# Seven products in place of eight in the FFN's first matmul of a two-layer trunk

## The chip, the core and the metric

The kernel runs on one core of a Trainium2 chip. The metric is the device time of one execution in microseconds; the time given for a kernel is the median of its runs. A profile belongs to one more execution, taken by the hardware profiler. In it PE is TensorE's matmuls, PEld its weight loads, DVE VectorE, ACT ScalarE, POOL GpSimd, and SP the engine whose queue issues most transfers.

## The reference

Two layers of attention and a gated FFN on 512 tokens of width 1024, all in float32. The change is in the FFN of each layer and in the final norm behind it:

```python
    h2 = rms_norm(x, g_ffn)
    gate, up = jnp.split(h2 @ w_ffn_in, 2, axis=-1)       # 1024 -> 2 x 2816
    return x + (jax.nn.silu(gate) * up) @ w_ffn_out       # 2816 -> 1024
...
    return rms_norm(x, norm_final)
```

## The kernel before

Everything is held transposed: channels on the 128 partitions, the 512 tokens along the free axis. The residual x is eight tiles `xs[0..7]` of 128 x 512. To keep float32 precision each operand is split in a rounded part and a remainder (`hi`, `lo`, fp32r), and each contraction tile takes three matmuls (`mm_tiles`, L205 to L207): hi by hi, lo by hi, hi by lo, all into one PSUM bank of 512 columns.

Weights come in one stream (`stream`, in the order of `layer_order`, L82 and L83). For each weight tile `w_pieces` issues a transfer of 512 KB on SP's queue into `wr` (three buffers), a cast on ScalarE into `wh` (L111) and a subtraction on VectorE into `wl` (L113; four buffers each). `w_get` hands out the next tile and keeps two ahead (`W_AHEAD`).

After attention the output projection adds into `xs`, and `Norm.feed` makes the scaled `hh` and `hl` of each tile and sums its squares; the reciprocal root r (one value a token) comes later from `Norm.finish`, and is multiplied in behind the matmuls, since it commutes with them. Then, in each layer:

- The FFN's first product (L623 to L640): 22 hidden tiles j, each with a gate product `fg` and an up product `fu` of 8 contraction tiles x 3 matmuls of 512 columns. VectorE multiplies both by r (L632, L634), ScalarE applies silu (L633), GpSimd multiplies (L635), and ScalarE and VectorE split the result into `ah` and `al` (L638, L639). All 22 pairs are kept.
- The FFN's second product (L644 to L651): output tiles m, each 22 contraction tiles x 3 matmuls into one bank, the weights in three tiles (1024, 1024 and 768 columns); VectorE adds the bank into `xs[m]` (L648).
- In the last layer output tile 7 is made in three stretches of 256, 128 and 128 tokens (L654 to L673). Behind each come the squares, two `ones_d` matmuls for the mean square (L666, L667), the reciprocal root (L152 to L156), eight multiplications on VectorE and GpSimd (L672) and the stores (L673).

Banks go round by `fbank` through eight PSUM banks. Each engine takes its instructions from a queue in order; the order across the program is made by a planner that follows the program's order of issue and its own estimate of when operands are there. The inputs' layout is made on the host, outside the time.

Of the kernel before, what the change touches and what calls it, by code (L numbers as in the profile page):

```python
# [35 lines left out]
BANK_BUFS = dict(mm=3, at=5)  # L36
W_BUFS, W_AHEAD = 4, 2
GATES_IN_BLK = 4
FILL = (3, 3, 3, 3, 4, 4, 4, 4)
LAG = 2  # L40


def f32(ap):
    return ap.bitcast(F32)
# [3 lines left out]
def trunk(ctx: ExitStack, tc, xT, par, tab, scn, msk, w_in, w_o, w_out, w_fi, w_fo, out):  # L48
# [7 lines left out]
    def bank(tag, name):  # L56
        return psm.tile([P, 512], F32, name=name, tag=tag, bufs=BANK_BUFS[tag])
# [24 lines left out]
    layer_order += [("fi", j) for j in range(2 * NH)]  # L82
    layer_order += [("fo", m, c) for m in range(8) for c in range(3)]  # L83
    stream = [(l,) + k for l in range(DEPTH) for k in layer_order]

    def w_src(k):
        l, kind, i = k[:3]
        if kind == "fo":
            c0, c1 = k[3] * 1024, min(k[3] * 1024 + 1024, HID)
            return w_fo[l, i][:, c0:c1]  # L90
        return {"in": w_in, "o": w_o, "out": w_out, "fi": w_fi}[kind][l, i]

    ready = []
# [2 lines left out]
    def w_pieces(*steps):  # L96

        n = state["next"]
        state["next"] = n + 1
        src = w_src(stream[n])  # L100
        cols = src.shape[1]
        raw = wp.tile([P, 1024], F32, name=f"wr{n}", tag="wr", bufs=3)
        hi = wp.tile([P, 1024], F32R, name=f"wh{n}", tag="wh", bufs=W_BUFS)
        lo = wp.tile([P, 1024], F32R, name=f"wl{n}", tag="wl", bufs=W_BUFS)
        ready.append((stream[n], hi, lo))
        at = 0
        for n_cols in steps:
# [6 lines left out]
            yield  # L114

    def w_prefetch():
        for _ in w_pieces(1024):
            pass

    def w_get(*key):  # L120
        while len(ready) <= W_AHEAD and state["next"] < len(stream):
            w_prefetch()
        k, hi, lo = ready.pop(0)
        assert k == key, (k, key)
        return hi, lo
# [69 lines left out]
    def mm(dst, key, rhs, first=True, last=True):  # L195

        hi, lo = w_get(*key)
        mm_tiles(dst, hi, lo, rhs, first, last)

    def mm_tiles(dst, hi, lo, rhs, first, last, c0=0):  # L200
        n = len(rhs)
        for k in range(n):
            rh, rl = rhs[k]
            c = slice((c0 + k) * P, (c0 + k + 1) * P)
            nc.tensor.matmul(dst, hi[:, c], rh, start=first and k == 0, stop=False)  # L205
            nc.tensor.matmul(dst, lo[:, c], rh, start=False, stop=False)  # L206
            nc.tensor.matmul(dst, hi[:, c], rl, start=False, stop=last and k == n - 1)  # L207
# [61 lines left out]
    def fbank(name):  # L269
        t = free_tags[fcount[0] % len(free_tags)]  # L270
        fcount[0] += 1
        return bank(t, name)

    for l in range(DEPTH):
        h = nrm.h
        with ExitStack() as ac:
# [337 lines left out]
            for m in range(8):  # L614
# [2 lines left out]
                nc.vector.tensor_tensor(out=xs[m], in0=b, in1=xs[m], op=ALU.add)  # L617
                nrm.feed(m)
        h = nrm.h
        with ExitStack() as fc:  # L620
            fp = fc.enter_context(tc.tile_pool(name=f"ffn{l}", bufs=1))
            act = []
            for j in range(NH):  # L623
                bg = fbank(f"fg{j}_{l}")
                mm(bg, (l, "fi", 2 * j), h)
                bu = fbank(f"fu{j}_{l}")
                mm(bu, (l, "fi", 2 * j + 1), h)
                if j == 0:
                    r = nrm.finish()
                g = fp.tile([P, S], F32, name=f"g{j}_{l}", tag="g", bufs=3)  # L630
                u = fp.tile([P, S], F32, name=f"u{j}_{l}", tag="u", bufs=3)
                nc.vector.tensor_tensor(out=g, in0=bg, in1=r, op=ALU.mult)  # L632
                silu = nc.scalar.activation(out=g, in_=g, func=AF.Silu)  # L633
                nc.vector.tensor_tensor(out=u, in0=bu, in1=r, op=ALU.mult)  # L634
                nc.gpsimd.tensor_tensor(out=u, in0=u, in1=g, op=ALU.mult)  # L635
                hi = fp.tile([P, S], F32R, name=f"ah{j}_{l}", tag="a", bufs=2 * NH)
                lo = fp.tile([P, S], F32R, name=f"al{j}_{l}", tag="a", bufs=2 * NH)
                nc.scalar.copy(out=hi, in_=u)  # L638
                nc.vector.tensor_tensor(out=lo, in0=u, in1=f32(hi), op=ALU.subtract)  # L639
                act.append((hi, lo))  # L640
            table(LNEXP, silu)
            last = l == DEPTH - 1
            nrm = Norm(C_NL if last else C_NA + 8 * (l + 1), f"a{l + 1}", split=not last)
            for m in range(7 if last else 8):  # L644
                b = fbank(f"fo{m}_{l}")
                for c in range(3):
                    mm(b, (l, "fo", m, c), act[8 * c:8 * c + 8], c == 0, c == 2)
                nc.vector.tensor_tensor(out=xs[m], in0=b, in1=xs[m], op=ALU.add)  # L648
                nrm.feed(m)
                if last:  # L650
                    nc.scalar.activation(out=xs[m], in_=xs[m], func=AF.Copy, scale=pt[:, C_NL + m:C_NL + m + 1])  # L651
            if last:

                w7 = [w_get(l, "fo", 7, c) for c in range(3)]  # L654
                for t, (t0, t1) in enumerate(((0, 256), (256, 384), (384, 512))):
                    ts, n = slice(t0, t1), t1 - t0
                    b = fbank(f"fo7{t}")
                    for c, (hi, lo) in enumerate(w7):
                        a = [(u[:, ts], v[:, ts]) for u, v in act[8 * c:8 * c + 8]]
                        mm_tiles(b[:, :n], hi, lo, a, c == 0, c == 2)  # L660
                    x7 = xs[7][:, ts]
                    nc.vector.tensor_tensor(out=x7, in0=b[:, :n], in1=x7, op=ALU.add)
                    sq = fp.tile([P, n], F32, name=f"sq7{t}", tag="g", bufs=3)
                    nc.scalar.activation(out=sq, in_=x7, func=AF.Square)
                    ms = bank("at", f"ms7{t}")
                    nc.tensor.matmul(ms[:, :n], ones_d, nrm.acc[:, ts], start=True, stop=False)  # L666
                    nc.tensor.matmul(ms[:, :n], ones_d, sq, start=False, stop=True)  # L667
                    nc.scalar.activation(out=x7, in_=x7, func=AF.Copy, scale=pt[:, C_NL + 7:C_NL + 8])
                    r = rsqrt_of(lambda name: rp.tile([P, n], F32, name=name, tag="r"), ms[:, :n], f"z{t}")
                    for m in range(8):  # L670
                        eng = nc.gpsimd if m in (0, 2, 4) else nc.vector
                        eng.tensor_tensor(out=xs[m][:, ts], in0=xs[m][:, ts], in1=r, op=ALU.mult)  # L672
                        (nc.scalar if m % 2 else nc.sync).dma_start(out=out[m][:, ts], in_=xs[m][:, ts])  # L673

# [52 lines left out]
```

## Time and profile before

| | us |
|---|---|
| runs of the kernel before: median (lowest to highest of 3) | 1513.78 (1513.16 to 1515.3) |
| the profiled execution | 1513.47 |
| span of its instructions | 1511.6 |
| TensorE busy in the span | 1484.6 |
| VectorE, ScalarE, GpSimd busy | 843.6, 615.5, 336.7 |

A matmul's duration in the records is modelled and covers its passage through the array; matmuls overlap, so what one costs in a run of them is the distance between two starts. A wait is put down to the semaphore that came last.

### The profile page before, as it was taken

Reading aid. Unit: us, or ns where it says so; the run is one execution under the profiler, and the core shown is the slowest. Engines: PE = TensorE matmul, PEld = TensorE weight load, DVE = VectorE, ACT = ScalarE, POOL = GpSimd, SP = SyncE. Lnnn points to the kernel's source line nnn. Section 1 sums busy time; section 2 is a strip of 40 time slices with the busy share of each in tenths; the row PEclk is TensorE's granted clock in tenths of the full one; section 3 lists DMA queues with packets and bytes.
Section 4 is the critical chain, followed back from the end, with each engine's and each line's share of the span. In section 5 each row is a group of like instructions: output and inputs, shape, how many; then the busy total and the mean of one; then the engine's idle time right before and its main releaser. Section 6 shows DMA issues by size and latency. Waiting matters only on the chain.

```text
span 1511.6 us, 17712 instructions
## 1 busy us (share of the span) xinstructions
PE 1484.6 (98%) x6954; PEld 1237.3 (82%) x6954; DVE 843.6 (56%) x1020; ACT 615.5 (41%) x974; POOL 336.7 (22%) x222
## 2 busy tenths in 40 slices
PE   9899999999999999999998999999999999999997
PEld 7788888888888888888876878888888888888887
DVE  6978776575454545432358776665645454443223
ACT  6556554643322233322345655446343333332321
POOL 2464652001111111101124454510021111110111
PEclk9999999999999999999999999999999999999999
DMA  6122232233223232333321123322322223233321
GB/s 251 44 79 66 78 101 81 71 110 98 98 98 98 92 103 86 97 93 105 110 82 57 63 78 98 98 70 87 109 98 84 100 95 98 97 94 93 100 77 57
DMA packets 44772, 139.61 MB, mean 92 GB/s; under 512 B 5776, under 2 KB 9232, under 8 KB 44688
## 3 DMA queue, kind: packets, MB, share of 16 engines
q1 hardware_dynamic: 42816, 137.39, 28.1%
q10 hardware_dynamic: 1872, 1.09, 0.2%
q8 instruction: 55, 0.90, 0.2%
q14 instruction: 29, 0.24, 0.1%
HBM read 132.16 MB, written 2.10 MB: 89 GB/s over the span
## 4 chain that ended last, share of the span: by engine, by line
PE 89%; DVE 5%; ACT 2%; issue 1%; DMA 1%; POOL 1%; SPq 1%; DVEq 0%; POOLq 0%; ACTq 0%
PE fo L205 5%; PE fo L206 5%; PE fo L207 5%; PE fg L206 5%; PE fu L206 5%; PE fu L205 5%; PE fg L205 5%; PE fu L207 5%; PE fg L207 5%; PE pg L205 4%; PE pg L206 4%; PE pg L207 4%; PE pd L205 2%; PE pd L206 2%; PE pd L207 2%; PE wo L207 2%
## 5 line engine op out<-in xcount | busy, mean ns | idle before, releaser
L111 ACT CAST wh<-wr 128x1024 fp32r<-128x1024 f32 (+3 forms) x251 | 258.1, 1029 | 632.1 <-issue 186.4
L113 DVE TENSOR_TENSOR wl<-wr,wh 128x1024 fp32r<-128x1024 f32 (+2 forms) x229 | 327.4, 1430 | 208.3 <-ACT wh L111 207.9
L635 POOL TENSOR_TENSOR u<-u,g 128x512 f32<-128x512 f32 x44 | 56.8, 1291 | 441.5 <-DVE u L634 394.3
L205 PE MATMUL fo<-ah,wh 128*128 128x512 f32 (+2 forms) x396 | 146.8, 371 | 0.0
L206 PE MATMUL fo<-ah,wl 128*128 128x512 f32 (+2 forms) x396 | 146.8, 371 | 0.0
L207 PE MATMUL fo<-al,wh 128*128 128x512 f32 (+2 forms) x396 | 146.7, 370 | 0.0
L205 PE MATMUL fg<-hhf,wh 128*128 128x512 f32 x352 | 137.7, 391 | 0.0
L207 PE MATMUL fu<-hlf,wh 128*128 128x512 f32 x352 | 136.9, 389 | 0.0
L206 PE MATMUL fg<-hhf,wl 128*128 128x512 f32 x352 | 136.9, 389 | 0.0
L207 PE MATMUL fg<-hlf,wh 128*128 128x512 f32 x352 | 136.9, 389 | 0.0
L205 PE MATMUL fu<-hhf,wh 128*128 128x512 f32 x352 | 136.9, 389 | 0.0
L206 PE MATMUL fu<-hhf,wl 128*128 128x512 f32 x352 | 136.9, 389 | 0.0
L634 DVE TENSOR_TENSOR u<-fu,yf 128x512 f32<-128x512 f32 x44 | 30.4, 691 | 129.2 <-PE fu L207 129.2
L205 PE MATMUL pg<-hha,wh 128*128 128x512 f32 x256 | 101.0, 394 | 0.0
L207 PE MATMUL pg<-hla,wh 128*128 128x512 f32 x256 | 100.2, 392 | 0.0
L206 PE MATMUL pg<-hha,wl 128*128 128x512 f32 x256 | 100.2, 391 | 0.0
L207 PEld LDWEIGHTS fo<-al,wh 128*128 128x128 f32 x396 | 74.6, 188 | 13.0
L206 PEld LDWEIGHTS fo<-ah,wl 128*128 128x128 f32 x396 | 74.6, 188 | 12.9
L205 PEld LDWEIGHTS fo<-ah,wh 128*128 128x128 f32 x396 | 74.6, 188 | 12.9
L205 PEld LDWEIGHTS fg<-hhf,wh 128*128 128x128 f32 x352 | 66.1, 188 | 14.3 <-issue 0.5
L206 PEld LDWEIGHTS fg<-hhf,wl 128*128 128x128 f32 x352 | 66.1, 188 | 14.0 <-issue 0.5
L207 PEld LDWEIGHTS fu<-hlf,wh 128*128 128x128 f32 x352 | 66.1, 188 | 13.7
(270 smaller groups left out, 3067.0 us busy)
## 6 DMA issues: line engine op xcount, KB each, us to landing
wr<-in_w_fi_dram SPq DMA_DIRECT2D x88, 512.0 KB, 3.3
wr<-in_w_in_dram SPq DMA_DIRECT2D x78, 512.0 KB, 3.3
wr<-in_w_fo_dram SPq DMA_DIRECT2D x32, 512.0 KB, 3.5
wr<-in_w_o_dram SPq DMA_DIRECT2D x16, 512.0 KB, 3.4
wr<-in_w_out_dram SPq DMA_DIRECT2D x16, 512.0 KB, 3.3
wr<-in_w_fo_dram SPq DMA_DIRECT2D x16, 384.0 KB, 3.1
x<-in_xT_dram SPq DMA_DIRECT2D x8, 256.0 KB, 5.9
cs<-in_tab_dram SPq DMA_DIRECT2D x2, 512.0 KB, 4.3
```

The lines of the kernel that those rows point to most:

```text
L111: nc.scalar.copy(out=hi[:, c], in_=raw[:, c])
L113: state["wl"] = eng.tensor_tensor(out=lo[:, c], in0=raw[:, c], in1=f32(hi[:, c]), op=ALU.subtract)
L205: nc.tensor.matmul(dst, hi[:, c], rh, start=first and k == 0, stop=False)
L206: nc.tensor.matmul(dst, lo[:, c], rh, start=False, stop=False)
L207: nc.tensor.matmul(dst, hi[:, c], rl, start=False, stop=last and k == n - 1)
L634: nc.vector.tensor_tensor(out=u, in0=bu, in1=r, op=ALU.mult)
L635: nc.gpsimd.tensor_tensor(out=u, in0=u, in1=g, op=ALU.mult)
```

## The change

In eleven of the 22 hidden tiles of each layer (`FAST`: 3, 5, 7, 8, 10, 11, 13, 14, 16, 17, 19) gate and up are computed together as a 2 x 2 block product: two output blocks (gate, up) by two halves of the tokens (`H` = 256 columns), over two halves of the contraction (even and odd tiles of 128 channels: `EVEN_ODD`, for which the host permutes the rows of `w_fi`). The Strassen-Winograd scheme makes the four results from seven block products and sums.

- Sums of the activations, once a layer: for four pairs of tiles, two scalings on ScalarE, three sums of 256 columns on VectorE and one on GpSimd, then one cast and one subtraction of 1024 columns (`sh`, `sl`).
- Sums of the weights, for each fast tile (`w_sums`): the two transfers of 512 KB as before, four subtractions of 512 columns on GpSimd in a chain (result `tf`, one buffer), and casts and subtractions of three tiles of 1024 and one of 512 columns, where an ordinary hidden tile has two of 1024. A fast tile counts as two in the look-ahead.
- The products (`Fast`, `prod`): 4 contraction tiles x 3 matmuls of 256 columns each. The bank `r0` takes b11 a11, then t2 s2, then t3 s3, then t4 a22, each on top of the last, and ScalarE copies it out after each of the first three (`snap`); `r2` takes t1 s1 and later b22 s4; `r1` takes b21 a12. VectorE adds copies to banks to make gate and up, GpSimd multiplies half of the gate by r. The last two products (`tail`) run after the first product of the next tile.
- The product of silu and up reads the up bank in PSUM on VectorE in an ordinary tile (no multiplication by r), and runs on GpSimd in a fast one. r is multiplied in behind the second product instead (`add_x`, two VectorE operations where one was).
- The second product goes in parts of the hidden tiles (`CHUNKS`): 0 to 5 after hidden tile 6, 6 to 11 after hidden tile 12, and 12 to 21 (two weight tiles of 640 columns, `ENDS`) at the end. Each part is added into `xs` by itself. Fourteen buffers hold `ah` and `al` where 44 did.
- In the last layer output tiles 6 and 7 are made in two halves of 256 tokens, in place of tile 7 alone in 256, 128 and 128.

The core of the diff:

```diff
+CHUNKS = ((0, 6), (6, 12), (12, 17), (17, NH))
+ENDS = (2, 3)
+FAST = (3, 5, 7, 8, 10, 11, 13, 14, 16, 17, 19)
+EVEN_ODD = (0, 2, 4, 6, 1, 3, 5, 7)
...
+    def w_sums():
...
+        pool, tag, bufs = (wp, "wr", 3) if j % 2 else (fp, "wx", 2)
+        rg = pool.tile([P, 2, 512], F32, name=f"rg{n}", tag=tag, bufs=bufs)
+        ru = pool.tile([P, 2, 512], F32, name=f"ru{n}", tag=tag, bufs=bufs)
+        for t, i in ((rg, 2 * j), (ru, 2 * j + 1)):
+            nc.sync.dma_start(out=t.rearrange("p a k -> p (a k)"), in_=w_fi[l, i])
+        tf = fp.tile([P, 3, 512], F32, name=f"tf{n}", tag="tf", bufs=1)
...
+        g = parts(rg, wp, "wh", W_BUFS, [P, 2, 512])
+        tt(nc.gpsimd, tf[:, 0], ru[:, 0], rg[:, 0])
+        tt(nc.gpsimd, ru[:, 0], ru[:, 1], ru[:, 0])
+        tt(nc.gpsimd, tf[:, 1], ru[:, 1], tf[:, 0])
+        tt(nc.gpsimd, tf[:, 2], rg[:, 1], tf[:, 1])
+        t = parts(tf[:, 0:2], fp, "ta", 2, [P, 2, 512])
+        u = parts(ru, wp, "wh", W_BUFS, [P, 2, 512])
+        v = parts(tf[:, 2], fp, "tb", 2, [P, 512])
...
+            for i in range(4):
+                he, ho = F("g", f"he{i}", 2), F("u", f"ho{i}", 2)
...
+                nc.vector.tensor_tensor(out=sf[:, 0], in0=he[:, H:], in1=ho[:, H:], op=ALU.add)
+                nc.gpsimd.tensor_tensor(out=sf[:, 2], in0=he[:, :H], in1=he[:, H:], op=ALU.subtract)
+                nc.vector.tensor_tensor(out=sf[:, 1], in0=sf[:, 0], in1=he[:, :H], op=ALU.subtract)
+                nc.vector.tensor_tensor(out=sf[:, 3], in0=ho[:, :H], in1=sf[:, 1], op=ALU.subtract)
...
+            def prod(dst, w, a, first=False):
+                hi, lo = w
+                for k, (ah, al) in enumerate(a):
+                    c = slice(k * P, k * P + P)
+                    for x, y, n in ((hi, ah, 0), (lo, ah, 1), (hi, al, 2)):
+                        nc.tensor.matmul(dst, x[:, c], y, start=first and k + n == 0,
+                                         stop=n == 2 and k == len(a) - 1, skip_group_check=True)
...
+                def __init__(self, j):
...
+                    prod(self.r0, self.w["b11"], A["a11"], True)
+                    self.a = self.snap("a")
...
+                def middle(self):
...
+                    prod(self.r2, w["t1"], A["s1"], True)
+                    prod(self.r0, w["t2"], A["s2"])
+                    b = self.snap("b")
+                    prod(r1, w["b21"], A["a12"], True)
...
+                    nc.vector.tensor_tensor(out=self.g[:, :H], in0=r1, in1=self.a, op=ALU.add)
+                    nc.gpsimd.tensor_tensor(out=self.g[:, :H], in0=self.g[:, :H], in1=r[:, :H], op=ALU.mult)
+                    prod(self.r0, w["t3"], A["s3"])
+                    c = self.snap("c")
+                    nc.vector.tensor_tensor(out=self.u[:, H:], in0=self.r2, in1=c, op=ALU.add)
...
+                def tail(self):
+                    w = self.w
+                    prod(self.r0, w["t4"], A["a22"])
+                    nc.vector.tensor_tensor(out=self.g[:, H:], in0=self.r0, in1=r[:, H:], op=ALU.mult)
+                    prod(self.r2, w["b22"], A["s4"])
+                    nc.vector.tensor_tensor(out=self.u[:, :H], in0=self.r2, in1=self.b, op=ALU.add)
+                    return hidden(self.j, self.g, self.u)
...
+            def add_x(b, m, ts=slice(0, S)):
...
+                nc.vector.tensor_tensor(out=t, in0=b, in1=r[:, ts], op=ALU.mult)
+                nc.vector.tensor_tensor(out=x, in0=t, in1=x, op=ALU.add)
...
+                for t, (t0, t1) in enumerate(((0, H), (H, S))):
...
+                    for m in (6, 7):
...
+                        eng = nc.gpsimd if m in ((0, 2, 3, 5, 6), (0, 2, 4))[t] else nc.vector
```

## Rows read from the trace of the kernel before

**Rows 1.** The page, first part: busy time, share of the span, instructions.

```profile
PE 1484.6 (98%) x6954; PEld 1237.3 (82%) x6954; DVE 843.6 (56%) x1020; ACT 615.5 (41%) x974; POOL 336.7 (22%) x222
```

**Rows 2.** The page, fourth part: the chain that ended last, by engine.

```profile
PE 89%; DVE 5%; ACT 2%; issue 1%; DMA 1%; POOL 1%; SPq 1%; DVEq 0%; POOLq 0%; ACTq 0%
```

**Rows 3.** Stretch: length, busy us of PE, PEld, DVE, ACT, POOL; clock, DMA.

```profile
391.92:424.56 32.64, 32.64 (x144) 26.68 (x143) 16.85 (x19) 12.79 (x16) 2.59 (x2) 1.00 0.29 92
60.00:520.00 460.00, 454.11 (x2164) 379.40 (x2163) 293.52 (x367) 212.57 (x360) 128.30 (x75) 1.00 0.27 86
1478.45:1486.37 7.92, 7.92 (x68) 7.91 (x67) 1.38 (x2) 1.35 (x2) 0.00 (x0) 1.00 0.01 2
```

**Rows 4.** Timeline of TensorE (start, duration): 24 matmuls of 512 columns apart.

```profile
561.44 0.39 PE L205 MATMUL fu<-hhf,wh 128*128 128x512 f32 x1
...
566.88 0.39 PE L205 MATMUL fg<-hhf,wh 128*128 128x512 f32 x1
```

**Rows 5.** The same: first matmul of layer 0's FFN, first of layer 1.

```profile
391.92 0.39 PE L205 MATMUL fg<-hhf,wh 128*128 128x512 f32 x1
...
751.84 0.39 PE L205 MATMUL p<-hha,wh 128*128 128x512 f32 x1
```

**Rows 6.** The same: 66 matmuls of 256 columns; 21 of 128.

```profile
1478.45 0.28 PE L205 MATMUL fo<-ah,wh 128*128 128x256 f32 x1
...
1486.37 0.59 PE L666 MATMUL ms<-acca,ones_d 128*128 128x256 f32 x2
...
1487.08 0.27 PE L205 MATMUL fo<-ah,wh 128*128 128x128 f32 x1
...
1489.42 0.27 PE L205 MATMUL fo<-ah,wh 128*128 128x128 f32 x1
```

**Rows 7.** Timeline of the end: last FFN matmul; final multiplications of two parts.

```profile
1492.55 3.38 DVE L672 TENSOR_TENSOR x<-x,yz 128x256 f32<-128x256 f32 x5
...
1502.25 0.27 PE L207 MATMUL fo<-al,wh 128*128 128x128 f32 x1
...
1506.83 1.88 DVE L672 TENSOR_TENSOR x<-x,yz 128x128 f32<-128x128 f32 x5
```

**Rows 8.** The page, sixth part: transfers of FFN weights, size, us to landing.

```profile
wr<-in_w_fi_dram SPq DMA_DIRECT2D x88, 512.0 KB, 3.3
```

**Rows 9.** Groups by line and shape: busy, mean ns of one, idle before.

```profile
L111 ACT CAST wh<-wr 128x1024 fp32r<-128x1024 f32 x230 | 242.1, 1053 | 563.2 <-issue 186.4 <-PE fg L207 113.8 <-PE fo L207 89.5
L635 POOL TENSOR_TENSOR u<-u,g 128x512 f32<-128x512 f32 x44 | 56.8, 1291 | 441.5 <-DVE u L634 394.3 <-ACT g L633 47.2
L632 DVE TENSOR_TENSOR g<-fg,yf 128x512 f32<-128x512 f32 x44 | 30.4, 692 | 65.4 <-PE fg L207 65.3
...
L664 ACT ACTIVATE sq<-x 128x256 f32<-128x256 f32 x1 | 0.4, 417 | 6.2 <-DVE x L662 6.2
L662 DVE TENSOR_TENSOR x<-fo,x 128x256 f32<-128x256 f32 x1 | 0.4, 425 | 5.8 <-PE fo L207 5.8
L672 POOL TENSOR_TENSOR x<-x,yz 128x256 f32<-128x256 f32 x3 | 2.7, 935 | 25.5 <-DVE yz L156 25.5
```

**Rows 10.** Waits of TensorE (total, times, longest), and the tile waited for.

```profile
PE avs L469 <- DVE tls L438: 6.7, 6, 2.2
...
L438 DVE TENSOR_TENSOR tls<-ts,ths x48: 402/676/693, 78.0 to 912.7; 128x512 fp32r<-128x512 f32 x32, 128x256 fp32r<-128x256 f32 x16
```

**Rows 11.** Timeline of GpSimd and VectorE in an ordinary hidden tile.

```profile
567.94 1.29 POOL L635 TENSOR_TENSOR u<-u,g 128x512 f32<-128x512 f32 x1 [9.59 <-DVE u L634]
...
568.21 2.10 DVE L113 TENSOR_TENSOR wl<-wr,wh 128x1024 fp32r<-128x1024 f32 x1 [0.44 <-ACT wh L111]
...
573.65 1.23 DVE L113 TENSOR_TENSOR wl<-wr,wh 128x1024 fp32r<-128x1024 f32 x1 [0.44 <-ACT wh L111]
```

**Rows 12.** The same two at the start of the FFN.

```profile
383.47 0.75 DVE L174 SCALAR_TENSOR_TENSOR hlf<-x,pt,hhf 128x512 fp32r<-128x512 f32 x1
...
383.52 1.84 POOL L188 TENSOR_TENSOR accf<-accf,sqf 128x512 f32<-128x512 f32 x1 [3.60 <-ACT sqf L186]
```

More of the change, by code (lines that the diff above doesn't have):

```diff
@@ L81, in trunk @@
     layer_order += [("o", m) for m in range(8)] + [("out", m) for m in range(8)]
-    layer_order += [("fi", j) for j in range(2 * NH)]
-    layer_order += [("fo", m, c) for m in range(8) for c in range(3)]
+    FFN = []
+    for j in range(NH):
+        FFN.append(("j", j))
+        FFN += [("c", c) for c, (j0, j1) in enumerate(CHUNKS) if j1 == j and c not in ENDS]
+    for kind, i in FFN:
+        if kind == "c":
+            layer_order += [("fo", m, i) for m in range(8)]
+        elif i not in FAST:
+            layer_order += [("fi", 2 * i), ("fi", 2 * i + 1)]
+        else:
+            layer_order.append(("fs", i))
+    layer_order += [("fo", m, c) for c in ENDS for m in range(2)] + [("fo", m, c) for m in range(2, 8) for c in ENDS]
     stream = [(l,) + k for l in range(DEPTH) for k in layer_order]
@@ L120, in w_get @@
     def w_get(*key):
-        while len(ready) <= W_AHEAD and state["next"] < len(stream):
+        while state["next"] < len(stream):
+            ahead = sum(2 if r[0][1] == "fs" else 1 for r in ready[1:])
+            if ready and ahead >= W_AHEAD:
+                break
             w_prefetch()
@@ L619, in trunk @@
         h = nrm.h
+        nrm_f = nrm
         with ExitStack() as fc:
[L621 to L632, printed above, removed]
-                silu = nc.scalar.activation(out=g, in_=g, func=AF.Silu)
[L634 to L640, printed above, removed]
@@ new lines, in trunk, with hidden @@
+            act = {}
+            last = l == DEPTH - 1
+            def hidden(j, g, u):
+                silu = nc.scalar.activation(out=g, in_=g, func=AF.Silu)
+                p = F("p", f"p{j}", 2)
+                (nc.vector if u.space == bass.MemoryType.PSUM else nc.gpsimd).tensor_tensor(
+                    out=p, in0=u, in1=g, op=ALU.mult)
+                if j < NH - 3:
+                    hi, lo = F("a", f"ah{j}", 14, dt=F32R), F("a", f"al{j}", 14, dt=F32R)
+                else:
+                    tag, bufs = (("tah", 2), ("tal", 2), ("sh0", 1))[j - NH + 3]
+                    t = F(tag, f"ae{j}", bufs, (P, 2, S), F32R)
+                    hi, lo = t[:, 0], t[:, 1]
+                nc.scalar.copy(out=hi, in_=p)
+                nc.vector.tensor_tensor(out=lo, in0=p, in1=f32(hi), op=ALU.subtract)
+                act[j] = (hi, lo)
+                return silu
@@ new lines, in add_x @@
+            def add_x(b, m, ts=slice(0, S)):
+                x = xs[m][:, ts]
+                t = F("p", f"ft{m}", 2)[:, ts]
+                nc.vector.tensor_tensor(out=t, in0=b, in1=r[:, ts], op=ALU.mult)
+                nc.vector.tensor_tensor(out=x, in0=t, in1=x, op=ALU.add)
+            late = []
+            for kind, i in FFN:
+                if kind == "j" and i not in FAST:
+                    bg = fbank(f"fg{i}_{l}")
+                    mm(bg, (l, "fi", 2 * i), hq)
+                    for o in late:
+                        silu = o.tail()
+                    late = []
+                    bu = fbank(f"fu{i}_{l}")
+                    mm(bu, (l, "fi", 2 * i + 1), hq)
+                    if i == 0:
+                        r = nrm_f.finish()
+                    g = F("g", f"g{i}", 2)
+                    nc.vector.tensor_tensor(out=g, in0=bg, in1=r, op=ALU.mult)
+                    silu = hidden(i, g, bu)
+                elif kind == "j":
+                    f = Fast(i)
+                    for o in late:
+                        o.tail()
+                    f.middle()
+                    late = [f]
+                else:
+                    for m in range(8):
+                        b = fbank(f"fo{m}{i}_{l}")
+                        mm(b, (l, "fo", m, i), [act[j] for j in range(*CHUNKS[i])])
+                        add_x(b, m)
@@ L641, in trunk, with finished @@
+            assert not late
             table(LNEXP, silu)
-            last = l == DEPTH - 1
             nrm = Norm(C_NL if last else C_NA + 8 * (l + 1), f"a{l + 1}", split=not last)
[L644 to L649, printed above, removed]
-                if last:
-                    nc.scalar.activation(out=xs[m], in_=xs[m], func=AF.Copy, scale=pt[:, C_NL + m:C_NL + m + 1])
+            def finished(m, ts=slice(0, S), square=True):
+                if square:
+                    nrm.feed(m)
+                if last:
+                    x = xs[m][:, ts]
+                    nc.scalar.activation(out=x, in_=x, func=AF.Copy, scale=pt[:, C_NL + m:C_NL + m + 1])
@@ new lines, in trunk @@
+            head = [fbank(f"fo{m}e_{l}") for m in range(2)]
+            for i in ENDS:
+                for m, b in enumerate(head):
+                    mm(b, (l, "fo", m, i), [act[j] for j in range(*CHUNKS[i])], i == ENDS[0], i == ENDS[-1])
+            for m in range(6 if last else 8):
+                if m < 2:
+                    b = head[m]
+                else:
+                    b = fbank(f"fo{m}e_{l}")
+                    for i in ENDS:
+                        mm(b, (l, "fo", m, i), [act[j] for j in range(*CHUNKS[i])], i == ENDS[0], i == ENDS[-1])
+                add_x(b, m)
+                finished(m)
@@ L652, in trunk @@
             if last:
-                w7 = [w_get(l, "fo", 7, c) for c in range(3)]
-                for t, (t0, t1) in enumerate(((0, 256), (256, 384), (384, 512))):
+                ws = {(m, i): w_get(l, "fo", m, i) for m in (6, 7) for i in ENDS}
+                for t, (t0, t1) in enumerate(((0, H), (H, S))):
                     ts, n = slice(t0, t1), t1 - t0
[L657 to L669, printed above, removed]
@@ new lines, in trunk @@
+                    for m in (6, 7):
+                        b = fbank(f"fo{m}{t}")[:, :n]
+                        for i in ENDS:
+                            a = [(act[j][0][:, ts], act[j][1][:, ts]) for j in range(*CHUNKS[i])]
+                            mm_tiles(b, *ws[m, i], a, i == ENDS[0], i == ENDS[-1])
+                        add_x(b, m, ts)
+                        sq = F("p", f"sq{m}{t}", 2)[:, :n]
+                        nc.scalar.activation(out=sq, in_=xs[m][:, ts], func=AF.Square)
+                        if m < 7:
+                            acc = nrm.acc[:, ts]
+                            nc.vector.tensor_tensor(out=acc, in0=acc, in1=sq, op=ALU.add)
+                            finished(m, ts, False)
@@ L670, in trunk @@
+                    ms = bank("at", f"ms7{t}")[:, :n]
+                    nc.tensor.matmul(ms, ones_d, nrm.acc[:, ts], start=True, stop=False)
+                    nc.tensor.matmul(ms, ones_d, sq, start=False, stop=True)
+                    finished(7, ts, False)
+                    rz = rsqrt_of(lambda name: rp.tile([P, n], F32, name=name, tag="r"), ms, f"z{t}")
                     for m in range(8):
-                        eng = nc.gpsimd if m in (0, 2, 4) else nc.vector
-                        eng.tensor_tensor(out=xs[m][:, ts], in0=xs[m][:, ts], in1=r, op=ALU.mult)
@@ L673, in trunk @@
-                        (nc.scalar if m % 2 else nc.sync).dma_start(out=out[m][:, ts], in_=xs[m][:, ts])
+                        eng = nc.gpsimd if m in ((0, 2, 3, 5, 6), (0, 2, 4))[t] else nc.vector
+                        eng.tensor_tensor(out=xs[m][:, ts], in0=xs[m][:, ts], in1=rz, op=ALU.mult)
+                        (nc.scalar if m % 2 and t else nc.sync).dma_start(out=out[m][:, ts], in_=xs[m][:, ts])
 def _tiles(np, w, kt, nt):
```

50 lines of the change are left out of this document (47 added, 3 removed).

## The prediction

> **What bounds the kernel now.** I read the page first: TensorE is busy 98% of the span while VectorE is at 56% and GpSimd at 22% [rows 1], and the chain that ended last lies on TensorE for 89% [rows 2]. Then the busy times by stage: in the first three hidden tiles of a layer TensorE is busy for all 32.64 us, VectorE for 16.85, ScalarE for 12.8, GpSimd for 2.6 [rows 3]. So in this stage the kernel is as fast as its matmuls follow one another, and only fewer or shorter matmuls help. The pace comes from the timeline, as the distance of starts (the durations shown are modelled and overlap). With 512 columns, 24 matmuls take from 561.44 to 566.88: 0.2267 us each [rows 4]; a layer's whole FFN, 391.92 to 751.84, holds 1584 matmuls and gives 0.2272 [rows 5], so nothing stalls there. With 256 columns, in the first part of output tile 7, 66 matmuls take 1478.45 to 1486.37: 0.120 us. With 128 columns 21 take 2.34 us: 0.111 [rows 6]. So half the columns cost 53% and a quarter 49%.
>
> **The change, term by term.** The sum starts at the profiled run, 1513.47 us, which lies 0.3 under the median of the runs.
>
> **Seven products.** An ordinary hidden tile has 2 x 8 x 3 = 48 matmuls of 512 columns: 48 x 0.2267 = 10.88 us. A fast one has 7 products of 4 contraction tiles, three matmuls each, of 256 columns: 84 x 0.120 = 10.08 us. That is 0.80 us for each of 22 fast tiles: -17.6 us. An eighth fewer columns would be 1.36 us; the rest goes to the 13 ns that each matmul costs above its columns at 2.4 GHz (0.120 against 256/2.4 = 0.107, 0.2267 against 0.2133), now paid 84 times, not 48. The granted clock is 1.00 in the FFN and in the stretch of 256 columns alike [rows 3], the upper of its two levels. By the Trainium skill (TensorE: Matmul & The Clock Gate, Back-to-back issue gap: N/2.4 + 2.5 ns) the saving would be 48 x 215.8 - 84 x 109.2 ns = 1.19 us a tile, 26 in all. The rows show 11 ns more at both widths, so I keep 17.6.
>
> **The end.** Before, output tiles 6 and 7 of the last layer take from 1478.45 - 66 x 0.2267 = 1463.49 to the last product's end at about 1502.36 [rows 6, 7]: 38.9 us, most of it 132 matmuls of 128 columns at the price of 256. Now 72 of their matmuls go to the early parts at 512 columns (16.3 us), the rest is 120 of 256 columns (14.4), and about 1.0 of the mean-square products stands between: 31.7. That is -7.2 us. What follows the last product was 1511.6 - 1502.4 = 9.2 us on 128 columns and is now on 256: the five multiplications of VectorE 3.38 us, not 1.88 [rows 7]; one more VectorE operation of 0.42; by 1.04 ns a column (0.692 against 0.425 us for 512 and 256 in the groups of costs below) 0.13 more for the first and for each of three operations of the reciprocal root; estimated in the same way, 0.1 for each of ScalarE's three, 0.3 for the mean-square matmuls and 0.2 for the last store. Sum 1.5 + 0.42 + 0.5 + 0.3 + 0.3 + 0.2 = +3.2 us (2 to 4).
>
> **The second FFN product in parts.** The matmuls are the same in number and width. It adds, for each output tile, part sums into the residual: three times two VectorE operations of 0.69 where one was. In the first two parts an output tile lasts 18 x 0.2267 = 4.1 us on TensorE and asks VectorE for 1.4 us and one weight remainder, narrower than an ordinary tile's; so it is hidden. There are 32 weight transfers a layer where there were 24, all smaller; two ahead is 6.8 us of TensorE (2 x 15 matmuls) in the last part against 3.3 us to landing [rows 8] and at most 2.3 of splitting (a cast and a remainder of 1024 columns, 1.05 and 1.23, in the groups below): hidden, cost 0. Without that cover each part tile would wait up to 5.6 - 3.4 = 2.2 us.
>
> **Short reads between products.** Three products of a fast tile accumulate on the same bank, and ScalarE copies the bank out in between (0.42 us for 256 columns, as VectorE's [rows 9]). After the first copy two or three other products follow; the second copy has one product (12 x 0.120 = 1.44 us) of cover, the third one product when a fast tile follows and the 5.4 us of a gate product when an ordinary one does. If ScalarE is just inside a cast of 1024 columns (1.05 us [rows 9]) the copy is late: 1.05 + 0.42 and the hand-over either way exceed 1.44. The queue is in order, so a cast that waits there for GpSimd also holds the copy; and on TensorE the waiting product holds all that is queued behind it. The trace has no such read; the nearest are the evacuations of the transposes in attention, of which TensorE waited for 6 of 48, 6.7 us in all, 0.14 us each [rows 10]. I take that for two tight reads of each fast tile: 44 x 0.14 = +6.2 us. Bounds: 0 (the product between covers all), and 1.5 us a fast tile, 33.
>
> **Start of the stage.** The sums of the activations are made while hidden tiles 0 to 2 run. VectorE was busy 16.85 of these 32.64 us [rows 3]; now come four times three operations of 0.42 and a remainder of 1.23 [rows 11], 10.0, and 1.9 for the remainders of a fast tile's weights in place of an ordinary one's: 28.7. ScalarE goes from 12.8 to about 24.5 (eight scalings of 512 columns at an estimated 0.7, between the 0.42 and the 1.05 of rows 9; four casts of 1.05; the extra weight casts 1.7). GpSimd has 8 us: four differences of a fast tile's weights at 1.29 and four of the activations at 0.7. So each fits, but if VectorE and GpSimd exclude each other all the time, 36.7 us do not, and the first fast tile is 4 us late. I take 1 us a layer, +2 us (0 to 8).
>
> **Steady load.** A fast tile asks ScalarE for about 6.2 of 10.08 us, no bound. VectorE: three remainders of 1.23 and two of 0.69, all with both inputs in SBUF, 5.07 us, and four operations from PSUM of 0.42, 1.7 us. GpSimd: four differences of 512 columns and one product at 1.29, and one of 256 columns (between 0.65, half of it, and 0.94 [rows 9]; I take 0.7), 7.15 us. An ordinary tile asks VectorE for 3.1 and 1.4 us and GpSimd for nothing, since its product now reads PSUM on VectorE. Two fast and an ordinary give TensorE 31.04 us, VectorE 18.0, GpSimd 14.3: each alone has room, so cost 0 on throughput. The weights of a fast tile are the same two transfers of 512 KB on SP's queue, which now start together. But the two don't run side by side: a remainder that takes 1.23 us takes 2.10 when GpSimd works beside it [rows 11], and GpSimd's 1.29 becomes 1.84 behind VectorE [rows 12]. The Trainium skill (SBUF — State Buffer, Who interferes with whom) says that a VectorE instruction with two SBUF inputs and a GpSimd instruction that reads SBUF exclude each other for a whole instruction, and one with a single SBUF input does not. The first half agrees with the 0.87 us added here; the second no row here shows.
>
> **Sum:** 1513.5 - 17.6 - 7.2 + 3.2 + 6.2 + 2 = 1500.1, so **1500 us**. Without any stall it is 1491.9.
>
> **Rivals.** *A, VectorE and GpSimd become the bound* because of that exclusion. In two fast tiles and an ordinary one 14.3 + 2 x 5.07 + 3.1 = 27.5 us exclude each other and 4.7 are VectorE's alone. If these never fall beside GpSimd's work the group needs 32.3 us against TensorE's 31.04: 1.2 us, some 11 groups, 13 us. With the stalls above: 1500 + 13 = 1513, no change. For it: the four differences are a chain and have one buffer for their results, so late work can't be made up early. Against it: VectorE's PSUM reads can lie beside GpSimd, and the two long early parts of the second FFN product let the queue empty. *B, slower:* the copies out of the bank stand behind casts that wait for that chain. A lost turn at the port costs one remainder, 1.23 us; if every fast tile loses one and TensorE waits it out, beside the 0.28 taken above, the stage pays 22 x 1.23 = 27 us: 1500 + 27 = 1527. It turns slower than before from 21.6/22 = 0.98 us of stall a fast tile. For it: one in-order queue holds both, and TensorE has 1.44 us of cover. Against it: the same engines feed attention and TensorE is busy 454 of 460 us there [rows 3]. *C, half the columns cost half* between products that change banks: 0.113 in place of 0.120, 22 x 84 x 7 ns = 12 us less, 1488. Against it: the 66 matmuls of rows 6 have the same form and a new weight tile each time. *D, the products are not fewer in effect:* if the order given to TensorE left it waiting for as long as it saves, only the end's 4.0 us would remain, 1509.5; that is the forecast's upper edge, no case of its own.
>
> **How the numbers follow.** Forecast (stalls from 0 to 0.8 us a fast tile, 1490 to 1510.5) 0.70; A 0.12; B 0.15; C 0.03. The range leaves out C and most of B: 1490 to 1517. A measurement of this kernel can tell some 0.2%, 3 us, from no change. Faster by more (under 1510.8): forecast, C and a part of A that has overlap, 0.78; the same 0.07; slower 0.15.
>
> **What would show it.** In the profile after: 12 matmuls of a product 1.44 us apart; the fast stretch with TensorE 95% busy or more and its waits on ScalarE's copies some 6 us in all; the remainders of VectorE near 2 us where GpSimd works; GpSimd busy about 70% there; after the last product some 12.4 us. I am wrong if the groups of two fast tiles and an ordinary one take much over 32 us, if the first fast tile starts late by several us, or if weights arrive late in the parts of the second product.

## The result, and the profile after

The changed kernel takes 1498.76 us (median; 1496.57 to 1500.28) against 1514.05 of the kernel before in the same runs: a ratio of 0.9899, 95% interval 0.9885 to 0.9913, so 1.0% less. The forecast was 1500. Its profiled execution took 1496.57 us, 16.9 under that of the kernel before, and its spans can be set side by side by stage. Each bound is the start of the first matmul of the next stage; the last stage begins where the first matmul of the last mean square follows the last product.

| stage, us | before | after | difference |
|---|---|---|---|
| start and attention of layer 0 | 391.92 | 390.99 | -0.93 |
| FFN of layer 0 | 359.92 | 351.53 | -8.39 |
| attention of layer 1 | 381.65 | 385.15 | +3.50 |
| FFN of layer 1, to its last product | 368.87 | 353.16 | -15.71 |
| from the last product to the end | 9.24 | 13.97 | +4.73 |
| span | 1511.6 | 1494.8 | -16.8 |

The bounds of layer 0's FFN after, as in [rows 5] before:

```profile
390.99 0.39 PE L259 MATMUL fg<-hhf,wh 128*128 128x512 f32 x1
...
742.52 0.39 PE L259 MATMUL p<-hha,wh 128*128 128x512 f32 x1
```

The first stage is the same code in both; its length lies between 391.0 and 393.3 us in the profiles of this case, so its difference says nothing. The sum of the forecast had 8.2 us of stalls in the FFN that are not there, and lacked 1.5 us at the end and 3.5 us of a stage that it left out. That it came out within 2 us is luck, since these cancel; the points below take it apart.

The page of the kernel after, first part and the granted clock of its second part:

```profile
PE 1461.4 (98%) x7670; PEld 1253.0 (84%) x7670; DVE 976.0 (65%) x1229; ACT 691.8 (46%) x1122; POOL 483.0 (32%) x317
...
PEclk9999999999999999999999999999999999999998
```

It answers [rows 1]: 716 more matmuls, yet TensorE is busy 23 us less; GpSimd does 146 us more, VectorE 132, ScalarE 76. The busy times by stretch (columns as in [rows 3]), first the three hidden tiles at the start of layer 0's FFN, then 40 us with fast and ordinary tiles:

```profile
391.00:423.60 32.60, 32.60 (x144) 26.66 (x142) 27.92 (x37) 22.94 (x30) 8.69 (x8) 1.00 0.35 114
600.00:640.00 40.00, 40.00 (x288) 37.84 (x287) 24.99 (x31) 16.82 (x26) 21.75 (x15) 1.00 0.24 80
```

TensorE is busy without a gap in both, as in [rows 3]. The waits of TensorE in the whole of layer 0's FFN, 391 to 742 us, are an empty list; so are those in layer 1's FFN up to 1480. What comes between the reads is seen in TensorE's timeline (the first matmul of each run, start and duration):

```profile
424.50 0.28 PE L725 MATMUL fa<-hhf,whh 128*128 128x256 f32 x1
...
425.94 0.28 PE L725 MATMUL fc<-sh,tah 128*128 128x256 f32 x1
...
427.38 0.28 PE L725 MATMUL fb<-hhf,whh 128*128 128x256 f32 x1
...
428.82 0.40 PE L259 MATMUL fg<-hhf,wh 128*128 128x512 f32 x1
429.05 0.28 PE L725 MATMUL fa<-sh,tah 128*128 128x256 f32 x1
...
430.49 0.40 PE L260 MATMUL fg<-hhf,wl 128*128 128x512 f32 x1
...
435.96 0.28 PE L725 MATMUL fa<-sh,whh 128*128 128x256 f32 x1
```

Each product of 12 matmuls lasts 1.44 us, as reckoned. But `fa`, the bank that ScalarE copies, is not taken up in the order of the code: the planner has put `fb` forward and the gate product of an ordinary tile (`fg`) in between. So in this first fast tile 3.1 us pass between the first and the second product on that bank (425.94 to 429.05), and 5.5 us between the second and the third (430.49 to 435.96), where the code order gives 1.44 for either. Over the 22 fast tiles the shortest such time is 2.88 us, two products.

### The profile page after: what moved, and what is told of

It is laid out like the page before. It is cut to its first block, busy times and chain, and to the rows that moved or that the text cites. A ratio compares the mean times of both kernels' runs of the same rounds, so it can differ in the third digit from the quotient of the medians.

```text
span 1494.8 us, 19780 instructions
## 1 busy us (share of the span) xinstructions
PE 1461.4 (98%) x7670; PEld 1253.0 (84%) x7670; DVE 976.0 (65%) x1229; ACT 691.8 (46%) x1122; POOL 483.0 (32%) x317
## 3 DMA queue, kind: packets, MB, share of 16 engines
q1 hardware_dynamic: 45120, 137.91, 28.7%
## 4 chain that ended last, share of the span: by engine, by line
PE 87%; DVE 6%; ACT 3%; issue 1%; POOL 1%; DMA 1%; SPq 0%; DVEq 0%; POOLq 0%; ACTq 0%
PE fa L725 8%; PE fc L725 4%; PE pg L259 4%; PE pg L260 4%; PE pg L261 4%; PE fo L259 3%; PE fo L260 3%; PE fo L261 3%; PE fg L259 3%; PE fg L260 3%; PE fu L261 3%; PE fg L261 3%; PE fu L260 3%; PE fu L259 3%; PE fb L725 2%; PE wo L259 2%
## 5 line engine op out<-in xcount | busy, mean ns | idle before, releaser
L127 ACT CAST wh<-wr 128x1024 fp32r<-128x1024 f32 (+4 forms) x223 | 213.8, 964 | 327.5 <-issue 55.3
L129 DVE TENSOR_TENSOR wl<-wr,wh 128x1024 fp32r<-128x1024 f32 (+3 forms) x201 | 247.6, 1236 | 77.4 <-ACT wh L127 75.9
L259 PE MATMUL fo<-ah,wh 128*128 128x512 f32 (+1 forms) x220 | 82.8, 376 | 0.0
L260 PE MATMUL fo<-ah,wl 128*128 128x512 f32 (+1 forms) x220 | 82.6, 375 | 0.0
L261 PE MATMUL fo<-al,wh 128*128 128x512 f32 (+1 forms) x220 | 82.3, 376 | 0.0
L259 PE MATMUL pd<-hha,wh 128*128 128x512 f32 x192 | 76.4, 398 | 0.3 <-ACT knd3s L404 0.3
L260 PE MATMUL pd<-hha,wl 128*128 128x512 f32 x192 | 76.2, 397 | 0.0
L261 PE MATMUL pd<-hla,wh 128*128 128x512 f32 x192 | 76.0, 396 | 0.0
L259 PE MATMUL fg<-hhf,wh 128*128 128x512 f32 x176 | 69.1, 393 | 0.0
L260 PE MATMUL fu<-hhf,wl 128*128 128x512 f32 x176 | 68.6, 390 | 0.0
```

## The experiments

**No fast tile.** All else of the change stays.

```diff
-FAST = (3, 5, 7, 8, 10, 11, 13, 14, 16, 17, 19)
+FAST = ()
...
-            for i in range(4):
+            for i in range(4 if FAST else 0):
```

> No hidden tile is fast; all else of the change stays (parts of 6, 6 and 10, last tiles by halves); the sums of the activations, which nothing reads then, are left out. If the seven products are worth their pace, 0.80 us a tile, and stand without stalls: FFN of layer 0 back from 351.5 to 360 us, the run 17 us above the changed kernel, near 1514. If stalls of 0.28 us a fast tile were in the changed kernel, only 0.52 a tile comes back: FFN of layer 0 at 357, the run near 1508. If the gain came from the parts of the second product, layer 0's FFN stays under 355.

Measured: 1512.02 us (median), ratio to before 0.9987 (0.9977 to 0.9996); the profiled span is 1510.0. Layer 0's FFN is 359.92, to the last digit that of the kernel before (start of its first matmul and of the next stage's first):

```profile
392.64 0.39 PE L259 MATMUL fg<-hhf,wh 128*128 128x512 f32 x1
...
752.56 0.39 PE L259 MATMUL p<-hha,wh 128*128 128x512 f32 x1
```

Layer 1's FFN is 361.53 where the changed kernel has 353.16. So eleven fast tiles are worth 8.39 and 8.37 us, 0.76 a tile where 0.80 was reckoned: the first theory, without stalls. The parts of the second product cost and give nothing in layer 0. In layer 1 the FFN without fast tiles is 7.34 us shorter than before: that is the end in two halves, reckoned at 7.2. Attention of layer 1 is 381.98 here, 3.2 less than in the changed kernel, though nothing in it was touched.

**Own buffers at the end.**

```diff
-rsqrt_of(lambda name: rp.tile([P, n], F32, name=name, tag="r"), ms, f"z{t}")
+rsqrt_of(lambda name: fp.tile([P, n], F32, name=name, tag="gu"[name[0] == "t"], bufs=2), ms, f"z{t}")
```

> Only the buffers of the last reciprocal root change: each half has its own pair, so that the second half's root no longer waits for the first half's five multiplications on GpSimd. If that wait is what made the end 4.7 us longer where 3.2 were reckoned, the time from the last product to the end falls from 14.0 by 1.4 (GpSimd still has the first half's work) to 2.3 us. If the end is long because of the stores or the wider operations alone, it stays at 14.0.

Measured: 1495.18 us (median); the end takes 11.83 us, not 13.97, all other stages but the first within 0.1 of the changed kernel's. In the changed kernel VectorE's queue at the end, and GpSimd's, read:

```profile
1487.20 0.42 DVE L208 SCALAR_TENSOR_TENSOR tz<-yz 128x256 f32<-128x256 f32 x1 [1.97 <-POOL x L847]
...
1483.12 4.05 POOL L847 TENSOR_TENSOR x<-x,yz 128x256 f32<-128x256 f32 x5 [13.80 <-DVE yz L210]
```

and with own buffers

```profile
1485.54 0.42 DVE L208 SCALAR_TENSOR_TENSOR tz<-yz 128x256 f32<-128x256 f32 x1 [2.19 <-ACT yz L207]
...
1480.36 4.26 POOL L847 TENSOR_TENSOR x<-x,yz 128x256 f32<-128x256 f32 x5 [10.60 <-DVE yz L210]
```

The second half's root starts on VectorE when GpSimd is through with the first half (1483.12 + 4.05), because the tag `r` has two buffers and each root takes two; with buffers of its own it starts when its operand is there.

**Which weights GpSimd splits.** The input projection's weights go to GpSimd where their number in the stream divides by four. A layer's stream had 124 weight tiles; the changed kernel's has 121 (a fast tile takes one place for two, the second product has eight more), so in layer 1 the choice falls on other weights.

```diff
-eng = nc.gpsimd if stream[n][1] == "in" and n % 4 == 0 else nc.vector
+eng = nc.gpsimd if stream[n][1] == "in" and n % len(layer_order) % 4 == 0 else nc.vector
```

> Which weights of the input projection are split on GpSimd is taken from the place in the layer, not in the whole stream; so layer 1 has the choice of the kernel before again (the change shortened a layer's stream from 124 to 121 weight tiles, and every fourth goes to GpSimd). If this moved choice makes layer 1's attention 3.5 us longer (385.15 against 381.65), it falls back to about 381.7, and the run by 3.5 us. If it is the planner's order after another FFN, or chance, it stays at 385.

Measured: 1494.54 us (median); attention of layer 1 is 382.20, 2.95 less than in the changed kernel and within 0.6 of the kernel before. Waits of TensorE in that stage of the changed kernel (742 to 1128 us; total, times, longest):

```profile
PE avs L523 <- DVE tls L492: 6.2, 4, 3.8
PE avs L522 <- ACT ths L491: 1.4, 2, 1.1
PE ts L488 <- POOL zs L511: 1.2, 1, 1.2
PE ts L488 <- ACT zs L506: 1.1, 1, 1.1
```

The largest is the one of [rows 10], an evacuation on VectorE. In the same stage of the kernel before (751 to 1134 us) it is

```profile
PE avs L469 <- DVE tls L438: 3.0, 3, 1.5
```

and with the choice put back it is 3.0 us again, in 3 waits. Other waits shift too: all of this stage's together are 7.9 us before, 9.9 after the change and 8.4 with the choice put back. How the choice leads to these waits was not followed. The profiles agree on the choice itself: a stream of 132 places (no fast tile), which divides by four like 124, gives 381.98, the other runs with 121 places and the old choice give 385.2 and 385.7, and the runs below with 115 places and the old choice give 388 to 390.

**All fast.** Hidden tiles 3 to 19, with no ordinary one between.

```diff
+FAST = tuple(range(3, 20))
```

> Hidden tiles 3 to 19 are all fast, with no ordinary one between. If TensorE stays the bound: 6 more tiles a layer at 0.80 us, FFN of layer 0 at 346.7, the run 9.6 us under the changed kernel. If VectorE and GpSimd exclude each other as reckoned (12.2 us of such work for a fast tile of 10.08): up to 20 us more in each layer's FFN, the run near 1530, GpSimd and VectorE together busy all the time there. If it is the short reads of ScalarE that ordinary products cover now: waits of TensorE on ScalarE's copies appear, 0.1 to 0.3 us for each of 28 to 34 reads a layer, 3 to 10 us.

Measured: 1528.61 us (median), ratio 1.0101 (1.0084 to 1.0118). Layer 0's FFN is 364.59, 13.1 above the changed kernel's with six fast tiles more, layer 1's 367.8. GpSimd's queue in one turn of a fast tile, and three of VectorE's operations in the same stretch:

```profile
644.24 1.29 POOL L144 TENSOR_TENSOR tf<-ru,rg 128x512 f32<-128x512 f32 x1 [1.23 <-DVE tbl L150]
645.49 2.27 POOL L706 TENSOR_TENSOR p<-u,g 128x512 f32<-128x512 f32 x1
647.72 1.30 POOL L144 TENSOR_TENSOR ru<-ru 128x512 f32<-128x512 f32 x1
648.98 1.75 POOL L144 TENSOR_TENSOR tf<-ru,tf 128x512 f32<-128x512 f32 x1
650.67 1.74 POOL L752 TENSOR_TENSOR g<-g,yf 128x256 f32<-128x256 f32 x1
652.37 2.27 POOL L144 TENSOR_TENSOR tf<-rg,tf 128x512 f32<-128x512 f32 x1
656.10 1.27 POOL L144 TENSOR_TENSOR tf<-ru,rg 128x512 f32<-128x512 f32 x1 [1.46 <-DVE tbl L150]
...
644.42 2.19 DVE L150 TENSOR_TENSOR whl<-rg,whh 128x1024 fp32r<-128x1024 f32 x1
649.49 0.41 DVE L755 TENSOR_TENSOR u<-fc,c 128x256 f32<-128x256 f32 x1
...
655.32 0.69 DVE L150 TENSOR_TENSOR tbl<-tf,tbh 128x512 fp32r<-128x512 f32 x1 [1.50 <-ACT tbh L149]
```

A turn is 656.10 - 644.24 = 11.86 us, near the 12.2 reckoned for work that excludes itself (called the shared way here: GpSimd's, and VectorE's with two inputs in SBUF), against 10.08 of TensorE. A GpSimd operation of 512 columns takes 1.29 or 2.27, a remainder of 1024 columns 1.22 at its shortest and 2.19 here. VectorE's addition with one input in PSUM (L755) keeps its 0.41 while GpSimd works beside it.

The lines also show a second part of the turn. GpSimd's six operations take 10.40 us (644.24 to 654.64), some 3.3 more than at their shortest (1.27 each, 0.73 for the one of 256 columns). Then GpSimd stands for 1.46 until VectorE's last remainder (`tbl`) has read `tf`, which has one buffer, and in part of that time neither engine works. So the turn is lengthening and this hand-over together; a second buffer for `tf` was not tried, and how much it would give is open.

The waits that this leaves on TensorE (391 to 760 us) name ScalarE first, which both theories would show:

```profile
PE fa L725 <- ACT c L740: 4.7, 4, 2.2
PE fc L725 <- ACT tah L149: 2.7, 3, 1.4
PE fa L725 <- DVE whl L150: 1.5, 1, 1.5
```

So two more runs were needed to tell the chain on GpSimd from short reads.

**All fast, without the chain on GpSimd.** The four differences are left out and the raw weights used in their place; all matmuls, casts, remainders and short reads stay.

```diff
-        tt(nc.gpsimd, tf[:, 0], ru[:, 0], rg[:, 0])
-        tt(nc.gpsimd, ru[:, 0], ru[:, 1], ru[:, 0])
-        tt(nc.gpsimd, tf[:, 1], ru[:, 1], tf[:, 0])
-        tt(nc.gpsimd, tf[:, 2], rg[:, 1], tf[:, 1])
-        t = parts(tf[:, 0:2], fp, "ta", 2, [P, 2, 512])
+        t = parts(rg, fp, "ta", 2, [P, 2, 512])
...
-        v = parts(tf[:, 2], fp, "tb", 2, [P, 512])
+        v = parts(ru[:, 0], fp, "tb", 2, [P, 512])
```

> Hidden tiles 3 to 19 all fast, as before, but the four differences of the weights on GpSimd are left out and the unsummed weights are split and used in their place, so the products are of other numbers; all matmuls, casts, remainders and short reads stay. If the exclusion of VectorE and GpSimd, with the chain on GpSimd, made that kernel slow, 7 us of such work are left for 10.08 us of TensorE, and layer 0's FFN falls from 364.6 to near 347. If the short reads by ScalarE between consecutive fast tiles made it slow, it stays above 355, with TensorE's waits on the copies.

Measured: 1491.44 us (median); layer 0's FFN 346.65 us, what the pace gives without any stall (346.7), and no wait of TensorE in it. Busy times of 600 to 640 us:

```profile
600.00:640.00 40.00, 40.00 (x336) 40.00 (x335) 25.35 (x34) 19.93 (x33) 6.84 (x7) 1.00 0.23 80
```

Between the second and the third product on a bank as little as 1.32 us passes in this layer, and no product waits. So the short reads cost nothing even with no ordinary tile between; the chain on GpSimd is what made all-fast slow, by its time on the shared way, its length with the one buffer, or both.

**All fast, the differences on VectorE.** The work stays, and only changes its engine.

```diff
-        tt(nc.gpsimd, tf[:, 0], ru[:, 0], rg[:, 0])
+        tt(nc.vector, tf[:, 0], ru[:, 0], rg[:, 0])
...
```

(and so for the other three)

> Hidden tiles 3 to 19 all fast with the four differences on VectorE (0.69 us each, 2.7 a tile) in place of GpSimd (1.29 each, 5.2). If the exclusion sets the pace, a fast tile's work on the shared way falls from 12.2 to 7.8 + 2.0 = 9.8 us and VectorE's own load is 9.5 of 10.08: layer 0's FFN between 347 and 355. If VectorE's load in its queue is as bad (its PSUM reads then stand behind the differences), it stays near 364.

Measured: 1496.68 us. Layer 0's FFN is 348.84 and layer 1's 349.61, 15.8 and 18.2 less than with the chain on GpSimd, though VectorE was the busier engine. Busy times of 600 to 640 us, first with the chain on GpSimd, then on VectorE:

```profile
600.00:640.00 40.00, 35.80 (x289) 34.70 (x288) 29.27 (x31) 18.79 (x30) 31.75 (x21) 1.00 0.27 93
```

```profile
600.00:640.00 40.00, 40.00 (x335) 40.00 (x334) 37.21 (x51) 22.49 (x34) 10.33 (x8) 1.00 0.25 86
```

With VectorE at 93% layer 0's FFN is 2.2 us longer than without the chain; with VectorE and GpSimd at 73% and 79% it is 18 longer. Not all of the 18 is waiting: TensorE's waits there add up to 12.4 us, and behind one of 2.16 us 15 matmuls of 256 columns (662.71 to 665.91) follow at 0.213 in place of 0.120, the lower level of the clock (256/1.2 GHz), which costs 1.4. The move takes the chain's operations from 1.27 us or more to a median of 0.68 as well as off GpSimd, so it doesn't part the shared way from the chain's length either. The remainders (min, median, max in ns) of layer 0's FFN, the changed kernel's first, then those of this run:

```profile
L150 DVE TENSOR_TENSOR whl<-rg,whh x11: 1219/1755/2317, 410.3 to 642.0; 128x1024 fp32r<-128x1024 f32 x11
L150 DVE TENSOR_TENSOR whl<-ru,whh x11: 1205/1695/1929, 418.3 to 649.2; 128x1024 fp32r<-128x1024 f32 x11
```

```profile
L150 DVE TENSOR_TENSOR whl<-rg,whh x17: 1209/1221/2319, 413.1 to 639.8; 128x1024 fp32r<-128x1024 f32 x17
L150 DVE TENSOR_TENSOR whl<-ru,whh x17: 1211/1219/1758, 419.5 to 646.4; 128x1024 fp32r<-128x1024 f32 x17
```

Their medians of 1.76 and 1.70 us become 1.22: the half microsecond between is lengthening beside GpSimd, and the profile counts it as busy time of VectorE.

**More work on GpSimd in the changed kernel.** Three of the four differences are done twice.

```diff
         tt(nc.gpsimd, tf[:, 0], ru[:, 0], rg[:, 0])
+        tt(nc.gpsimd, tf[:, 0], ru[:, 0], rg[:, 0])
...
         tt(nc.gpsimd, tf[:, 1], ru[:, 1], tf[:, 0])
+        tt(nc.gpsimd, tf[:, 1], ru[:, 1], tf[:, 0])
         tt(nc.gpsimd, tf[:, 2], rg[:, 1], tf[:, 1])
+        tt(nc.gpsimd, tf[:, 2], rg[:, 1], tf[:, 1])
```

> The changed kernel with three of the four differences of each fast tile's weights done twice on GpSimd, with the same result: 3.9 us more GpSimd work for each fast tile. If GpSimd and VectorE exclude each other, two fast tiles and an ordinary one ask for 27.5 + 7.7 = 35.3 us of such work against TensorE's 31.04, less what the two long parts of the second product take up: layer 0's FFN 8 to 23 us longer than 351.5. If each engine only has its own limit (GpSimd 14.3 + 7.7 = 22 of 31 us), it stays at 351.5.

Measured: 1537.97 us; layer 0's FFN 371.67, 20.1 more. Busy times of 600 to 640 us:

```profile
600.00:640.00 40.00, 34.40 (x210) 31.23 (x209) 23.34 (x24) 15.05 (x21) 34.28 (x22) 0.91 0.23 80
```

So in the mix of the change, too, 3.9 us more on GpSimd for a fast tile make TensorE wait, with GpSimd busy for 34.28 of 40 us and not full. Some 4 of the 20.1 us are again matmuls at the lower clock (0.91 granted in this stretch). The run lengthens the chain as well as the time on the shared way, so it doesn't part these two; that VectorE is the better place for the same chain is what the run before it shows.

**The two small mends together.** Own buffers at the end and the choice by place in the layer.

> The two small mends together: own buffers for the last reciprocal root (2.1 us in its run) and the choice of weights split on GpSimd by the place in the layer (3.0 us in its run). If they are separate, 5.1 us less than the changed kernel: the profiled run near 1491.5, the end at 11.8, layer 1's attention at 382.

Measured: 1492.70 us (median), ratio 0.9865 (0.9848 to 0.9881); attention of layer 1 382.06, the end 11.82, the profiled run 1491.50. They add up.

**All mends.** All-fast with the differences on VectorE, and the two small mends.

> Hidden tiles 3 to 19 all fast with the differences on VectorE, own buffers for the last reciprocal root, and the choice of weights split on GpSimd by the place in the layer. If the three are separate: FFN stages as in the run with the differences on VectorE (348.8 and 349.6), layer 1's attention 382 in place of 390.2, the end 11.8 in place of 14.0: the profiled run near 1486.5, 12 us under the changed kernel's median. If layer 1's attention is long there because of another order and not because of the choice, it stays near 390 and the run near 1494.

Measured: 1488.82 us (median; 1487.4 to 1490.1), ratio 0.9832 (0.9819 to 0.9846): 10 us under the changed kernel and the shortest of this case. Attention of layer 1 is 382.61, the FFN stages 348.85 and 350.24. The profiled run was 1490.1, 3.6 above what was expected of it: the first stage 393.25, which varies, and the end 13.25 where 11.8 was expected. There VectorE was still multiplying for the first half when the second half's last product was done:

```profile
1474.66 2.68 DVE L847 TENSOR_TENSOR x<-x,yz 128x256 f32<-128x256 f32 x3
1477.26 0.41 DVE L769 TENSOR_TENSOR ft<-fo,yf 128x256 f32<-128x256 f32 x1
```

L769 reads the last product, ready after 1474.95, at 1477.26; with own buffers alone the same step came 1.2 us earlier behind its product (1481.27 and 1482.41).

## Why the forecast was right, and which of its terms were not

**Seven products, -17.6: measured -16.8.** 8.39 + 8.37 us from the run without fast tiles. In layer 0 the 924 short matmuls take 110.7 us (0.1198 each); the 1056 others take 240.9 where the pace gives 239.4. Of these 1.5 us some 0.8 were there before the change (359.9 for 359.1 [rows 5]); the rest, most of it some 70 steps of 0.232 to 0.237 in place of 0.227 among the ordinary matmuls, is about the 0.4 us that a layer misses. The pace of the 256-column row [rows 6] held. The formula of the Trainium skill (TensorE: Matmul & The Clock Gate, Back-to-back issue gap) would have given 26 us; the page gives it for an isolated matmul and not for a stream of weight loads and matmuls such as this one.

**The end in halves, -7.2: measured -7.34** (layer 1's FFN of the kernel before, 368.87, less 361.53 without fast tiles).

**Behind the last product, +3.2: measured +4.73.** The terms of the wider operations were nearly right, and rather high: without the shared buffers the end is 11.83, +2.6, and there VectorE, still multiplying for the first half, takes up the last product 0.9 us later than in the changed kernel (1.14 us behind it, not 0.20). What failed is that I priced the end as one chain and not its buffers: five multiplications of the first half on GpSimd keep the pair of buffers that the second half's root wants. I had read the tag of two buffers in the code and not set it against the new assignment of GpSimd.

**Second product in parts, 0: measured 0.** 359.92 us in layer 0 with and without, fast tiles left out.

**Short reads, +6.2: measured 0.** The row that I took it from [rows 10] is of attention and of another kind of read, and it did not carry over. Here the planner puts other products between two on the same bank (the timeline after), 2.88 us or more. That was the step that failed: an order of issue in the code was taken for the order on the engine. The count was off as well: in seven of the eleven fast tiles an ordinary one stands before, and the first copy then has one product of cover in the code's order, not two or three. And a short cover need not cost: all-fast without the chain has times of 1.32 us and no wait.

**Start of the stage, +2: measured 0.** The load was reckoned well: VectorE 27.92 us (28.7), ScalarE 22.94 (24.5), GpSimd 8.69 (8). It fits, so it is hidden; the 1 us a layer was caution.

**Not in the sum: layer 1's attention, +3.5.** The change alters a count, and the choice of GpSimd or VectorE for weights of another stage hangs on that count. I compared no stage outside the FFN, though the line that chooses is in the part that the change leaves alone.

**Rival A (VectorE and GpSimd as the bound)** did not come in the changed kernel: of its 13 us none shows, since the mix stays under the bound (GpSimd 54% busy in the stretch shown, where I had expected about 70%, and no wait of TensorE). In all-fast a turn of 11.86 us for 12.2 reckoned fits its mechanism, but the one buffer of the chain, which the rival named, has its part in that turn, and no run parts the two. The exclusion agrees with the Trainium skill (SBUF — State Buffer, Who interferes with whom), now in both halves: operations with two SBUF inputs go from 1.23 to 2.2 us beside GpSimd, those with one input in PSUM keep 0.41. **Rival B** as priced did not come; TensorE's waits on the copies appear in all-fast, but go with the chain. **Rival C** is out: 0.1198 us a matmul. **Rival D** is out: 16.8 of 17.6 us came.

## What to carry to other kernels

When a change puts work on VectorE and GpSimd together, add up the time of GpSimd and of VectorE's operations with two SBUF inputs as if on one engine, and set that sum against the engine to be kept busy: here 27.5 of 31.0 us cost nothing, 12.2 of 10.08 cost 18 us in layer 0, and moving the chain to the engine that does it in half the time gave most of that back. It is a first reckoning: a chain with one buffer can bind by its length too, which these runs don't part from it. Read the waits of a bound engine with care: the copies named by TensorE were late because of a chain two engines away. And look for choices that hang on a running number: a change in one stage can move work in another.

## What the runs showed of the hardware

GpSimd's own operations are lengthened as VectorE's are: 512 columns take 1.27 us or up to 2.28 in all-fast, and VectorE's 1024 columns 1.22 or up to 2.32. An addition on VectorE that reads one operand from PSUM took 0.41 us inside a GpSimd operation that was running for 1.75. In all-fast and in the run with more work on GpSimd, where TensorE had waits, the granted clock fell in single stretches of the FFN: in the latter to 0.91 in 600 to 640 us, where TensorE stood still for 3.7 us up to 617.5 and for 1.9 up to 621.4, while it was 1.00 in the same stretch of the changed kernel, without waits. Waits alone did not bring it down everywhere: all-fast kept 1.00 in 600 to 640 us, with waits of at most 1.5 us.
